# A decoder layer on one core: weight pieces of 128x1024 in place of 128x512, gating in the gates' buffer, expert products kept in fours

## The chip, the cores and the metric

The kernel runs on one core of a Trainium2 chip. The metric is the device time of one execution in microseconds, and lower is better. TensorE (PE, with its weight loads as PEld), VectorE (DVE), ScalarE (ACT), GpSimd (POOL) and SyncE (SP) each run their own instructions in order and wait for one another by semaphores; DMA engines move data between the large memory (HBM) and the on-chip buffers SBUF and PSUM.

## The reference

One decoder layer on 1024 tokens of width 1024, in float32: a hybrid mixer (a gated convolution and a chunked delta rule), cross-attention into 256 memory tokens, and a mixture of 16384 one-neuron experts. The last part sets the size of the work:

```python
def peer_ffn(xn, w_query, sub_keys, expert_u, expert_v):
    ...
    idx = jnp.take_along_axis(cand_idx, pos, axis=-1)
    gates = jax.nn.softmax(best, axis=-1).astype(xn.dtype)
    ...
    def block(args):        
        xt, it, gt = args
        u = expert_u[it]
        v = expert_v[it]
        act = jax.nn.gelu(jnp.einsum("td,ted->te", xt, u), approximate=False)
        return jnp.einsum("te,ted->td", gt * act, v)
```

## The kernel before

The 1024 tokens are eight blocks of 128. They go through the layer in three chunks: `ca` (blocks 0 and 1, 256 tokens), `cb` (blocks 2 to 5, 512 tokens) and `cc` (blocks 6 and 7). The experts are done in two ways. Blocks 0, 1, 6 and 7 fetch the rows that each token chose by indirect DMA, one gather of 128 rows of 4 KB (512 KB) per slot, into a ring `g` of NG = 6 buffers: in `gather_u` VectorE multiplies each with the tokens and sums (line 926, 128 gathers a block, 512 in all), and in `gather_v` VectorE adds it, weighted, to `g_y` (line 1006, 3 blocks). Block 0 goes through `gather_p` instead: TensorE weights and adds the gathered rows. A gather there holds the 128 experts of one token; a pair of gathers is multiplied by two weight columns `W[:, c, u]` in two halves of 512 columns, which makes four products on line 963. The columns land in a strip of 32 of the 128 result rows. There are 64 pairs and 256 products, each of which stands twice in the trace (512 rows).

Blocks 2 to 5 go through all experts instead (`dense`): 32 groups of 512 experts, whose gates were written to the table `gd` in HBM. A group has, in each of its two halves, two calls of `hidden` (line 1066 loads the gates `gv`; a product of 128 experts with 512 tokens, gelu, gating, a split) and one of `output` for the group before it (four result banks, line 1093 adds them to `y`). A group has 192 matmuls of 128x512.

All big products are three matmuls of a split weight and a split input (`mm3`, lines 241 to 243). `load_w` is the path of each weight piece: SP's DMA writes `wraw` (line 233), ACT rounds it to `whi` (line 235), VectorE subtracts to get `wlo` (line 237), and of the three matmuls two read `whi` and one `wlo`. In `proj_ct` (channel-major products and `hidden`) the weights are the stationary operand, in `proj_tok` and `output` they are streamed. A piece is 128x512, so a 128x1024 block of weights is two pieces; there are 904 pieces, in rings of

```python
NSHORT, NRAW, NHI, NLO, NG, LU, LV, VD = 6, 6, 4, 3, 6, 1, 1, 194
```

six, four and three buffers of 2 KB a partition. A ring buffer is written again only when its last reader is done. In `hidden` the gelu goes from PSUM to a short buffer `d_s` (line 1072), VectorE multiplies it with the gates in place (line 1074), ACT rounds it (line 1075) and VectorE subtracts (line 1076); each of these is 128x512 and is done 128 times.

The program is written as generators that `merge` takes steps from in proportion: the gathers of blocks 0 and 1 beside the second chunk, the tables and the third chunk after that, and at the end

```python
run(merge((chain(ga, at('PG3', gathers(6))), 1036 - G1 - G2 - G3 - G4 - G5), (at("PD", dense(2 * P)), PACE)))
```

the remaining gathers beside the dense groups. A scheduler then puts the instructions of each engine into a fixed order by a simulated timeline, so an edit to one instruction can move others.

## Time and profile before

| | us |
|---|---|
| median of 3 runs (lowest, highest) | 3319.79 (3313.24, 3326.74) |
| the profiled execution | 3329.34 |
| its span in the trace | 3327.6 |
| TensorE busy | 2834.6 |
| VectorE busy | 2870.7 |
| POOL, ACT busy | 1275.5, 1169.5 |

The profiled execution is a single one, and 9.6 us longer than the median. Everything read from its trace is set against its own time; the 1.7 us around its span are taken as unchanged. [...] Instructions of one engine overlap a little: the next one on VectorE can start before the end of the one before, so a duration is longer than what an instruction takes from the engine.

### The profile page before, as it was taken

How to read it: one execution, taken by the hardware profiler on the slowest of the kernel's cores; microseconds unless marked ns; L12 is line 12 of the kernel's file. 1: busy time of each engine (PE TensorE's matmuls, PEld its weight loads, DVE VectorE, ACT ScalarE, POOL GpSimd, SP SyncE). 2: the span in 40 equal slices, each digit the busy share in tenths (PEclk: the TensorE clock that was granted, in tenths of full speed). 3: DMA queues.
4: the chain of work that ended last, by engine and by line, in shares of the span. 5: the costliest groups of instructions: out<-in, count | busy, mean ns of one | idle time of the engine just before them, and what ended most of it. 6: DMA issues, size and time to landing. Idle time of an engine off the chain costs nothing.

```text
span 3327.6 us, 45373 instructions
## 1 busy us (share of the span) xinstructions
PE 2834.6 (85%) x14826; PEld 2302.9 (69%) x14826; DVE 2870.7 (86%) x6291; ACT 1169.5 (35%) x2387; POOL 1275.5 (38%) x1028
## 2 busy tenths in 40 slices
PE   8898587868899879464566799899999999999996
PEld 8887566655555556463455677778888888888875
DVE  6665899977665698999999999989999999999996
ACT  5444343312133333333334343233333333333332
POOL 0000036635543433002656154544454454544440
PEclk9899789979999889786778899999999999999998
DMA  4344358948887877214889678999999999989993
GB/s 162 113 133 144 133 199 293 366 164 307 311 298 263 326 257 282 98 59 182 306 293 360 222 258 307 346 309 344 335 345 345 332 347 356 346 317 344 337 338 127
DMA packets 367054, 890.56 MB, mean 268 GB/s; under 512 B 34656, under 2 KB 103904, under 8 KB 362720
## 3 DMA queue, kind: packets, MB, share of 16 engines
q0 software_dynamic: 147456, 536.94, 45.1%
q1 hardware_dynamic: 219360, 350.72, 30.2%
q8 instruction: 116, 1.90, 0.2%
q14 instruction: 122, 1.00, 0.1%
HBM read 838.77 MB, written 48.76 MB: 267 GB/s over the span
## 4 chain that ended last, share of the span: by engine, by line
PE 56%; DVE 23%; DMA 8%; issue 7%; POOL 4%; ACT 2%; SPq 0%; DVEq 0%; POOLq 0%; ACTq 0%
PE ps L241 16%; PE ps L243 16%; PE ps L242 16%; DVE g L926 4%; POOL g L909 3%; DVE wlo L237 2%; PE ps L963 2%; DVE g_y L1006 1%; DMA g<-expert_u,g_ii 1%; DMA wraw<-expert_v 1%; DMA g<-expert_v,g_y 1%; DMA wraw<-u_t 1%; DVE t_s L810 1%; DVE unit L1039 1%; DMA d_s<-kmd 1%
## 5 line engine op out<-in xcount | busy, mean ns | idle before, releaser
L235 ACT ACTIVATE whi<-wraw 128x512 fp32r<-128x512 f32 x904 | 568.5, 632 | 1363.2 <-PE ps L242 599.4
L909 POOL DMA_INDIRECT g<-expert_u,g_ii x512 | 608.2, 1188 | 1020.0 <-DVE t_s L811 443.9
L243 PE MATMUL ps<-unit,wlo 128*128 128x512 f32 (+1 forms) x2144 | 774.6, 365 | 63.7 <-DVE wlo L237 63.6
L909 POOL DMA_INDIRECT g<-expert_v,g_ii x384 | 531.9, 1385 | 774.0 <-DVE g_y L1006 384.2
L237 DVE TENSOR_TENSOR wlo<-wraw,whi 128x512 fp32r<-128x512 f32 x904 | 622.5, 690 | 193.2 <-issue 55.0
L241 PE MATMUL ps<-unit,whi 128*128 128x512 f32 (+1 forms) x2144 | 780.2, 365 | 6.6 <-ACT whi L235 6.0
L242 PE MATMUL ps<-unit,whi 128*128 128x512 f32 (+1 forms) x2144 | 772.1, 361 | 7.9 <-DVE unit L289 7.9
L926 DVE SCALAR_TENSOR_TENSOR g<-g,xn 128x1024 f32<-128x1024 f32 x512 | 622.7, 1222 | 86.9 <-DMA g<-expert_u,g_ii 80.3
L242 PE MATMUL ps<-wlo,unit 128*128 128x512 f32 x1312 | 516.3, 394 | 15.8 <-DVE wlo L237 15.6
L243 PEld LDWEIGHTS ps<-unit,wlo 128*128 128x128 f32 x2144 | 420.9, 197 | 150.7 <-DVE wlo L237 84.7
L243 PE MATMUL ps<-whi,unit 128*128 128x512 f32 x1312 | 513.6, 392 | 0.0
L1006 DVE SCALAR_TENSOR_TENSOR g_y<-g,g_a,g_y 128x1024 f32<-128x1024 f32 x381 | 488.8, 1283 | 9.5 <-DMA g<-expert_v,g_ii 7.9
L241 PEld LDWEIGHTS ps<-unit,whi 128*128 128x128 f32 x2144 | 423.3, 198 | 75.6 <-ACT whi L235 14.3
L242 PEld LDWEIGHTS ps<-unit,whi 128*128 128x128 f32 x2144 | 422.5, 197 | 66.8 <-DVE unit L289 9.2
L241 PE MATMUL ps<-whi,unit 128*128 128x512 f32 x1312 | 411.5, 396 | 18.1 <-ACT whi L235 16.8
L241 PEld LDWEIGHTS ps<-whi,unit 128*128 128x128 f32 x1312 | 247.9, 189 | 79.7 <-ACT whi L235 20.2
L242 PEld LDWEIGHTS ps<-wlo,unit 128*128 128x128 f32 x1312 | 247.7, 189 | 78.4 <-DVE wlo L237 22.4
L243 PEld LDWEIGHTS ps<-whi,unit 128*128 128x128 f32 x1312 | 247.7, 189 | 55.1 <-issue 4.4
L955 POOL DMA_INDIRECT g<-expert_v,g_y x128 | 135.2, 1056 | 173.9 <-DVE g L926 45.4
L963 PE MATMUL ps<-g,g_y 128*32 128x512 f32 x512 | 132.2, 647 | 49.1 <-DMA g<-expert_v,g_y 49.0
L1093 DVE TENSOR_TENSOR unit<-ps,unit 128x512 f32<-128x512 f32 x248 | 162.4, 686 | 11.2 <-PE ps L243 10.9
L1045 PE MATMUL ps<-unit 128*128 128x128 f16 x1024 | 83.6, 239 | 61.0 <-DVE unit L1039 61.0
(276 smaller groups left out, 3062.5 us busy)
## 6 DMA issues: line engine op xcount, KB each, us to landing
wraw<-u_t SPq DMA_DIRECT2D x256, 256.0 KB, 5.5
wraw<-expert_v SPq DMA_DIRECT2D x256, 256.0 KB, 6.4
wraw<-w_in SPq DMA_DIRECT2D x168, 256.0 KB, 4.5
gd<-unit SPq DMA_DIRECT2D x32, 1024.0 KB, 7.9
unit<-gd SPq DMA_DIRECT2D x32, 1024.0 KB, 15.6
wraw<-w_out SPq DMA_DIRECT2D x48, 256.0 KB, 3.5
wraw<-w_xq SPq DMA_DIRECT2D x48, 256.0 KB, 3.9
wraw<-w_xo SPq DMA_DIRECT2D x48, 256.0 KB, 4.2
```

The costliest lines, as they stand in the source:

```text
L235: act(hi, raw, AF.Copy)
L237: tt(lo, raw, hi.bitcast(F32), op=OP.subtract)
L241: nc.tensor.matmul(ps, lh, rh, start=first, stop=False)
L242: nc.tensor.matmul(ps, lh, rl, start=False, stop=False)
L243: nc.tensor.matmul(ps, ll, rh, start=False, stop=last)
L909: nc.gpsimd.indirect_dma_start(out=g, out_offset=None, in_=I[table], in_offset=bass.IndirectOffsetOnAxis(ap=ii[:, k:k + 1], axis=0))
L926: stt(g, g, 1.0, xn, op0=OP.mult, op1=OP.mult, accum_out=r.a[:, k:k + 1])
L955: nc.gpsimd.indirect_dma_start(out=g, out_offset=None, in_=I["expert_v"], in_offset=bass.IndirectOffsetOnAxis(ap=iT[:, t:t + 1], axis=0))
L963: nc.tensor.matmul(acc[32 * cc:32 * cc + 32], W[:, c, u], gs[c][:, half * 512:(half + 1) * 512], start=q == 0 and u == 0, stop=q == 7 and ...
L1006: stt(y, g, a[:, k:k + 1], y, op0=OP.mult, op1=OP.add)
L1045: nc.tensor.matmul(ps[:, u * P:(u + 1) * P], part[i][:, g, :, t], oj[:, g, :, t], start=i == 0, stop=i == 1)
L1093: tt(dst, pss[b], dst, op=OP.add)
```

## The change

Four edits stand together.

1. `load_w` takes 128x1024 at once. There are 452 loads of 512 KB, 452 ACT roundings and 452 subtractions in place of 904 of each. The rings hold 3, 2 and 2 buffers of 4 KB. `proj_tok` and `output` take two row blocks of 512 columns in one load.
2. `hidden` does two blocks of 128 experts: gelu is written back to PSUM, the gating multiplies PSUM with the gates into the gates' buffer `gv`, and one rounding and one subtraction of 128x1024 follow for both.
3. In `gather_p` the four products of a pair of gathers begin with one that needs the later gather, and the other three are tied behind it (`tc.issue_after`).
4. A 128x128 matrix of ones became one column that is read as a broadcast (two small uses, left out of the diff below).

```diff
@@ -43,7 +43,7 @@
 G1, G2, G3, G4, G5 = 98, 90, 107, 17, 137
 A5 = -1
 C4, T5 = 61, 92
-NSHORT, NRAW, NHI, NLO, NG, LU, LV, VD = 6, 6, 4, 3, 6, 1, 1, 194
+NSHORT, NRAW, NHI, NLO, NG, LU, LV, VD = 6, 3, 2, 2, 6, 1, 1, 194
 PG1, PG2, PG3, PT, PR, PD = 100, -25, 0, 0, 0, 0
 
 
@@ -229,11 +229,11 @@
 
     def load_w(src):
 
-        raw = wp.tile([P, 512], F32, name="wraw", bufs=NRAW)
-        nc.sync.dma_start(raw, src)
-        hi = wp.tile([P, 512], F32R, name="whi", bufs=NHI)
+        raw = wp.tile([P, D], F32, name="wraw", bufs=NRAW)
+        nc.sync.dma_start(raw if len(src.shape) == 2 else raw.rearrange("p (a c) -> p a c", a=2), src)
+        hi = wp.tile([P, D], F32R, name="whi", bufs=NHI)
         act(hi, raw, AF.Copy)
-        lo = wp.tile([P, 512], F32R, name="wlo", bufs=NLO)
+        lo = wp.tile([P, D], F32R, name="wlo", bufs=NLO)
         tt(lo, raw, hi.bitcast(F32), op=OP.subtract)
         return hi, lo
 
@@ -296,13 +296,12 @@
 
         xhi, xlo = x
         ps = psum()
-        for g in range(2):
-            hi, lo = load_w(src[:, g * 512:(g + 1) * 512])
-            for j in range(4):
-                k = 4 * g + j
-                js = slice(j * P, (j + 1) * P)
-                mm3(ps[:, :nt], hi[:, js], lo[:, js], xhi[:, k, :nt], xlo[:, k, :nt], k == 0, k == KD - 1)
-            yield
+        hi, lo = load_w(src)
+        for k in range(KD):
+            js = slice(k * P, (k + 1) * P)
+            mm3(ps[:, :nt], hi[:, js], lo[:, js], xhi[:, k, :nt], xlo[:, k, :nt], k == 0, k == KD - 1)
+            if k % 4 == 3:
+                yield
         return ps[:, :nt]
 
     def proj_tok(wsrc, lhs, nblk, consume):
@@ -310,11 +309,14 @@
         for half in range(2):
             pss = [psum() for b in range(nblk)]
             for k in range(KD):
-                hi, lo = load_w(wsrc[k * P:(k + 1) * P, half * 512:(half + 1) * 512])
+                cs = slice(half * 512, (half + 1) * 512)
+                if k % 2 == 0:
+                    hi, lo = load_w(wsrc[k * P:(k + 2) * P, cs].rearrange("(a p) c -> p a c", a=2))
+                ks = slice((k % 2) * 512, (k % 2 + 1) * 512)
                 xh, xl = lhs(k)
                 for b in range(nblk):
                     bs = slice(b * P, (b + 1) * P)
-                    mm3(pss[b], xh[:, bs], xl[:, bs], hi, lo, k == 0, k == KD - 1)
+                    mm3(pss[b], xh[:, bs], xl[:, bs], hi[:, ks], lo[:, ks], k == 0, k == KD - 1)
                 yield
             for b in range(nblk):
                 consume(b, half, pss[b])
@@ -957,13 +959,18 @@
                         gs.append(g)
                         if c == 0:
                             yield
-                    for half in range(2):
-                        for c in range(2):
-                            cc = 2 * c + half
-                            nc.tensor.matmul(acc[32 * cc:32 * cc + 32], W[:, c, u],
-                                             gs[c][:, half * 512:(half + 1) * 512],
-                                             start=q == 0 and u == 0, stop=q == 7 and u == 3,
-                                             skip_group_check=True)
+                    def product(c, half):
+                        cc = 2 * c + half
+                        return nc.tensor.matmul(acc[32 * cc:32 * cc + 32], W[:, c, u],
+                                                gs[c][:, half * 512:(half + 1) * 512],
+                                                start=q == 0 and u == 0, stop=q == 7 and u == 3,
+                                                skip_group_check=True)
+
+
+                    with tc.issue_after(product(1, 0).ins):
+                        product(1, 1)
+                        product(0, 0)
+                        product(0, 1)
                     yield
             st = slip()
             act(st, acc, AF.Copy)
@@ -1066,22 +1073,28 @@
             nc.sync.dma_start(v, gd[:, :, 4 * g:4 * g + 4, :].rearrange("b i j t -> i b j t"))
             return v
 
-        def hidden(g, jj, hh, hl, gv):
-            ps = yield from proj_ct(I["u_t"][4 * g + jj], x, T)
-            a = short()[:, :T]
-            act(a, ps, AF.Gelu)
-            a3 = a.rearrange("p (b t) -> p b t", t=32)
-            tt(a3, a3, gv[:, :, jj, :], op=OP.mult)
-            act(hh[:, jj], a, AF.Copy)
-            tt(hl[:, jj], a, hh[:, jj].bitcast(F32), op=OP.subtract)
+        def hidden(g, j0, hh, hl, gv):
+
+            js = slice(j0, j0 + 2)
+            for jj in (j0, j0 + 1):
+                ps = yield from proj_ct(I["u_t"][4 * g + jj], x, T)
+                act(ps, ps, AF.Gelu)
+                tt(gv[:, :, jj, :], ps.rearrange("p (b t) -> p b t", t=32), gv[:, :, jj, :], op=OP.mult)
+            a = gv[:, :, js, :].rearrange("p b j t -> p j b t")
+            h4, l4 = (h[:, js].rearrange("p j (b t) -> p j b t", t=32) for h in (hh, hl))
+            act(h4, a, AF.Copy)
+            tt(l4, a, h4.bitcast(F32), op=OP.subtract)
 
         def output(g, half, hh, hl):
             pss = [psum() for _ in range(NB)]
             for jj in range(4):
-                vh, vl = load_w(ev[4 * g + jj][:, half * 512:(half + 1) * 512])
+                if jj % 2 == 0:
+                    vh, vl = load_w(ev[4 * g + jj:4 * g + jj + 2, :, half * 512:(half + 1) * 512]
+                                    .rearrange("j i c -> i j c"))
+                vs = slice((jj % 2) * 512, (jj % 2 + 1) * 512)
                 for b in range(NB):
                     bs = slice(b * P, (b + 1) * P)
-                    mm3(pss[b], hh[:, jj, bs], hl[:, jj, bs], vh, vl, jj == 0, jj == 3)
+                    mm3(pss[b], hh[:, jj, bs], hl[:, jj, bs], vh[:, vs], vl[:, vs], jj == 0, jj == 3)
                 yield
             if not y:
                 y.extend(rows(NB))
@@ -1099,8 +1112,7 @@
                 cur = (unit().bitcast(F32R), unit().bitcast(F32R), load_g(g))
             for half in range(2):
                 if cur:
-                    for jj in (2 * half, 2 * half + 1):
-                        yield from hidden(g, jj, *cur)
+                    yield from hidden(g, 2 * half, *cur)
                 if prev:
                     yield from output(g - 1, half, *prev[:2])
             prev = cur
```

How this stands on the engines is read at three places. The first is TensorE at the first products of block 0, beside the delta rule of the second chunk (lines 574 to 626, which are 576 to 628 after the change). `L963` is a product of a gathered pair (`L964` after). Before:

```order
L963 MATMUL ps<-g,g_y 32x512 x3
L595 MATMUL ps<-call,unit 128x128 x8
L963 MATMUL ps<-g,g_y 32x512
L605 MATMUL ps<-unit 128x128 x8
L614 MATMUL ps<-call,unit 128x128 x8
L963 MATMUL ps<-g,g_y 32x512 x3
L623 MATMUL ps<-unit 128x128 x4
L626 MATMUL ps<-unit 128x128 x4
L623 MATMUL ps<-unit 128x128 x3
L963 MATMUL ps<-g,g_y 32x512
L623 MATMUL ps<-unit 128x128
```

After the change:

```order
L964 MATMUL ps<-g,g_y 32x512 x4
L597 MATMUL ps<-call,unit 128x128 x8
L607 MATMUL ps<-unit 128x128 x8
L616 MATMUL ps<-call,unit 128x128 x8
L625 MATMUL ps<-unit 128x128 x2
L964 MATMUL ps<-g,g_y 32x512 x4
L625 MATMUL ps<-unit 128x128 x2
L628 MATMUL ps<-unit 128x128 x4
L625 MATMUL ps<-unit 128x128 x4
L628 MATMUL ps<-unit 128x128 x4
L964 MATMUL ps<-g,g_y 32x512 x4
```

The runs of one and of three products became runs of four. Over the whole program there were 91 runs before, 40 of them of one product, 30 of three and 7 of four; now there are 60, 36 of them of four, 8 of one and 7 of eight.

The second place is VectorE in the first dense groups, from the 444th of the 904 weight pieces on (the 222nd of 452 after the change). `L926` is the multiplication of a gathered row set of `expert_u` for blocks 6 and 7 (`L928` after), `L1006` the addition of one of `expert_v` (`L1013` after), `L885` and its neighbours belong to the routing of block 7, and `L1074` is the gating (`L1082` after). Before:

```order
L237 TENSOR_TENSOR wlo<-wraw,whi 128x512
L926 SCALAR_TENSOR_TENSOR g,g_a<-g,xn 128x1024
L1006 SCALAR_TENSOR_TENSOR g_y<-g,g_a,g_y 128x1024
L237 TENSOR_TENSOR wlo<-wraw,whi 128x512
L885 TENSOR_TENSOR t_s<-t_s,masks 128x1024
L1074 TENSOR_TENSOR d_s<-d_s,unit 128x512
L926 SCALAR_TENSOR_TENSOR g,g_a<-g,xn 128x1024
L237 TENSOR_TENSOR wlo<-wraw,whi 128x512
L1006 SCALAR_TENSOR_TENSOR g_y<-g,g_a,g_y 128x1024
L887 TENSOR_REDUCE p_s_19094<-t_s 128x64
L237 TENSOR_TENSOR wlo<-wraw,whi 128x512
L926 SCALAR_TENSOR_TENSOR g,g_a<-g,xn 128x1024
```

After the change:

```order
L237 TENSOR_TENSOR wlo<-wraw,whi 128x1024
L227 TENSOR_TENSOR rs_t<-rs_t,rs_x 128x1
L928 SCALAR_TENSOR_TENSOR g,g_a<-g,xn 128x1024
L887 TENSOR_TENSOR t_s<-t_s,masks 128x1024
L928 SCALAR_TENSOR_TENSOR g,g_a<-g,xn 128x1024
L237 TENSOR_TENSOR wlo<-wraw,whi 128x1024
L1082 TENSOR_TENSOR unit<-ps,unit 128x16x32
L928 SCALAR_TENSOR_TENSOR g,g_a<-g,xn 128x1024
L228 SCALAR_TENSOR_TENSOR rs_y<-rs_t,rs_y 128x1
L928 SCALAR_TENSOR_TENSOR g,g_a<-g,xn 128x1024
```

The gathered rows stand earlier in the order. Counted from the start of the program, 127 additions of `expert_v` rows stand before the 448th piece in both orders, but of multiplications of `expert_u` rows there were 259 and there are now 275; before the 496th piece there were 320, and there are now 347. Before the 424th piece, still ahead of block 7's rows, there were 112 additions and there are now 119. From the 472nd to the 736th piece the new order is 24 to 27 row sets ahead, counted over both kinds.

The third place is VectorE in the middle of the dense groups, where the two kinds of gathered row sets alternate with the weight pieces. Before (`L1074` and `L1076` are the gating and the split of `hidden`):

```order
L237 TENSOR_TENSOR wlo<-wraw,whi 128x512
L1074 TENSOR_TENSOR d_s<-d_s,unit 128x512
L926 SCALAR_TENSOR_TENSOR g,g_a<-g,xn 128x1024
L237 TENSOR_TENSOR wlo<-wraw,whi 128x512
L1076 TENSOR_TENSOR unit<-d_s,unit 128x512
L1006 SCALAR_TENSOR_TENSOR g_y<-g,g_a,g_y 128x1024
L926 SCALAR_TENSOR_TENSOR g,g_a<-g,xn 128x1024
L237 TENSOR_TENSOR wlo<-wraw,whi 128x512
L1074 TENSOR_TENSOR d_s<-d_s,unit 128x512
L237 TENSOR_TENSOR wlo<-wraw,whi 128x512
L1006 SCALAR_TENSOR_TENSOR g_y<-g,g_a,g_y 128x1024
```

After the change (`L1082` and `L1086` in their place):

```order
L237 TENSOR_TENSOR wlo<-wraw,whi 128x1024
L1082 TENSOR_TENSOR unit<-ps,unit 128x16x32
L928 SCALAR_TENSOR_TENSOR g,g_a<-g,xn 128x1024
L1013 SCALAR_TENSOR_TENSOR g_y<-g,g_a,g_y 128x1024
L928 SCALAR_TENSOR_TENSOR g,g_a<-g,xn 128x1024
L237 TENSOR_TENSOR wlo<-wraw,whi 128x1024
L1082 TENSOR_TENSOR unit<-ps,unit 128x16x32
L1013 SCALAR_TENSOR_TENSOR g_y<-g,g_a,g_y 128x1024
L1086 TENSOR_TENSOR unit<-unit 128x1024
L928 SCALAR_TENSOR_TENSOR g,g_a<-g,xn 128x1024
L237 TENSOR_TENSOR wlo<-wraw,whi 128x1024
L1013 SCALAR_TENSOR_TENSOR g_y<-g,g_a,g_y 128x1024
```

A subtraction is 128x1024 now and stands half as often, the gating reads PSUM, and the split of two blocks of experts is one instruction. On the other engines the order of these steps is the same in kind; the load of `gv` on SP stands after the last `expert_v` piece of a half-group, where it stood before the last `u_t` piece.

## Rows read from the trace of the kernel before

**Rows 1.** The page: busy time by engine, and its chain that ended last.
```profile
PE 2834.6 (85%) x14826; PEld 2302.9 (69%) x14826; DVE 2870.7 (86%) x6291; ACT 1169.5 (35%) x2387; POOL 1275.5 (38%) x1028
...
PE 56%; DVE 23%; DMA 8%; issue 7%; POOL 4%; ACT 2%; SPq 0%; DVEq 0%; POOLq 0%; ACTq 0%
```
**Rows 2.** Windows: length, busy us (instructions) by engine, clock, DMA share, GB/s.
```profile
core 0: us, PE busy (x) PEld busy (x) DVE busy (x) ACT busy (x) POOL busy (x), PEclk, DMA share, GB/s
0.00:332.00 332.00, 291.25 (x1980) 273.91 (x1981) 203.63 (x500) 167.02 (x379) 0.20 (x4) 0.96 0.41 138
500.00:665.00 165.00, 135.74 (x611) 105.67 (x609) 165.00 (x318) 56.13 (x108) 106.34 (x82) 0.95 0.93 329
747.00:1332.00 585.00, 516.73 (x2682) 341.44 (x2682) 417.42 (x1200) 180.91 (x393) 268.74 (x252) 0.92 0.83 292
1332.00:1910.00 578.00, 350.03 (x2595) 305.58 (x2593) 559.71 (x1497) 220.51 (x576) 179.81 (x105) 0.79 0.60 217
1910.00:2240.00 330.00, 311.47 (x1328) 250.79 (x1327) 310.15 (x582) 116.14 (x190) 165.62 (x119) 0.98 0.88 303
2240.00:3160.00 920.00, 918.82 (x4051) 759.90 (x4050) 864.03 (x1236) 302.49 (x514) 451.56 (x382) 1.00 0.96 341
```
**Rows 3.** Waits from 747 to 1332 us: total, times, longest.
```profile
POOL g L909 <- PE ps L963: 103.3, 29, 15.9
...
PE ps L963 <- DMA g<-expert_v,g_y: 49.0, 23, 6.4
```
**Rows 4.** Timeline of TensorE around two runs of products: start, length.
```profile
947.70 1.06 PE L963 MATMUL ps<-g,g_y 128*32 128x512 f32 x6
948.69 0.50 PE L242 MATMUL ps<-unit,whi 128*128 128x512 f32 x1
...
999.63 1.05 PE L963 MATMUL ps<-g,g_y 128*32 128x512 f32 x2
1000.61 0.33 PE L742 MATMUL ps<-call,d_s 128*128 128x128 f32 x1
```
**Rows 5.** Groups by line and form: count, busy us, mean ns, idle before.
```profile
L926 DVE SCALAR_TENSOR_TENSOR g<-g,xn 128x1024 f32<-128x1024 f32 x512 | 622.7, 1222 | 86.9 <-DMA g<-expert_u,g_ii 80.3 <-issue 5.3 <-DMA g<-expert_v,g_y 1.1
L237 DVE TENSOR_TENSOR wlo<-wraw,whi 128x512 fp32r<-128x512 f32 x904 | 622.5, 690 | 193.2 <-issue 55.0 <-ACT whi L235 45.9 <-PE ps L242 44.1
...
L1075 ACT ACTIVATE unit<-d_s 128x512 fp32r<-128x512 f32 x128 | 80.4, 628 | 129.0 <-DVE d_s L1074 128.0
...
L249 ACT ACTIVATE d_s<-unit 128x1024 bf16<-128x1024 f32 x24 | 25.2, 1058 | 9.5 <-DVE unit L334 5.1 <-DMA unit<-x 4.1
```
**Rows 6.** Timeline of VectorE in the dense groups: start, length.
```profile
2401.35 1.22 DVE L926 SCALAR_TENSOR_TENSOR g<-g,xn 128x1024 f32<-128x1024 f32 x1
2402.49 0.09 DVE L926 DVE_READ_ACCUMULATOR g<-g,xn 128x1 f32 x1
2402.49 0.69 DVE L237 TENSOR_TENSOR wlo<-wraw,whi 128x512 fp32r<-128x512 f32 x1
2403.09 1.28 DVE L1006 SCALAR_TENSOR_TENSOR g_y<-g,g_a,g_y 128x1024 f32<-128x1024 f32 x1
```
**Rows 7.** VectorE's subtractions for weight pieces in two stretches (busy, count).
```profile
500.00:665.00 165.00, 28.85 (x42) 0.95 0.93 329
1332.00:2240.00 908.00, 139.47 (x203) 0.86 0.70 248
```
**Rows 8.** The page, DMA issues: count, KB each, us to landing.
```profile
wraw<-u_t SPq DMA_DIRECT2D x256, 256.0 KB, 5.5
wraw<-expert_v SPq DMA_DIRECT2D x256, 256.0 KB, 6.4
...
unit<-gd SPq DMA_DIRECT2D x32, 1024.0 KB, 15.6
```
**Rows 9.** Waits from 2240 to 3160 us: total, times, longest.
```profile
ACT whi L235 <- DMA wraw<-u_t: 109.2, 15, 10.6
ACT unit L1075 <- DVE d_s L1074: 99.5, 57, 3.9
```

8 lines of the change are left out of this document (4 added, 4 removed).

## The prediction

> **What bounds the kernel now.** I read the page first: TensorE is busy 85% of the span and VectorE 86%, so neither is idle enough to be ignored, and the chain that ended last is 56% TensorE and 23% VectorE [rows 1]. An average hides which engine sets the pace where, so the windows come next [rows 2]. The reader should see four kinds of stretch. From 0 to 332 us TensorE works 291 of 332. From 500 to 665 VectorE is busy for all of the 165 us. From 747 to 1332, where block 0's products run, TensorE is the fullest (517 of 585; VectorE 417, DMA 0.83). From 1332 to 1910 VectorE is busy 560 of 578 and TensorE only 350. From 1910 to 2240 both are nearly full (311 and 310 of 330), and from 2240 to 3160 TensorE is busy 919 of 920: there nothing gains time unless it takes matmuls away, and the change takes none. So a gain has to come before 2240, and after 2240 one can only lose. Waits and timelines give the prices.
>
> **Products of block 0.** A run of six rows (three products) that starts at 947.70 is followed by the next matmul at 948.69, and a run of two rows (one product) at 999.63 by the next at 1000.61 [rows 4]. So a run costs 0.98 to 0.99 us whether it holds one product or three. That nothing else runs in most of it is what makes splitting dear. I count this 0.99 for each four products of a run or part of four, an estimate for the longer runs. By the order the old program has 91 runs with 107 such parts, 106 us; the new has 60 with 73, 72 us. TensorE is relieved of 34 us between 747 and 1332. How much comes through? TensorE is at 517/585 = 88% there, which would pass on some 30 us; but in the same stretch TensorE waits 49.0 us for gathered rows inside the runs and POOL waits 103.3 us for products to free a buffer of the ring [rows 3]. A run of four waits for the later of its two gathers and frees both buffers together, so a part of the relief turns into waiting. Bounds 0 and -34; I take two thirds, **-22**.
>
> **Half as many instructions on VectorE.** A subtraction of 128x512 lasts 690 ns, the nearest 128x1024 instruction of two inputs 1222 ns [rows 5]. In the timeline the subtraction that starts at 2402.49 is followed at 2403.09, the 128x1024 one of 2401.35 at 2402.49 [rows 6]: 0.60 and 1.14 us of the engine. A pair saves 2 x 0.60 - 1.14 = 0.06 us. Only stretches that VectorE sets count: 42 + 203 pieces [rows 7], 122 pairs, 7 us. Counted by durations a pair would save 2 x 690 - 1222 = 158 ns and the 122 pairs 19 us, but the starts say that most of this already overlaps the next instruction, and an engine that is full goes by starts. Bounds 0 and -19, taken **-7**. [...] In the dense groups a gating pair drops one more instruction (two splits of 0.60 become one of 1.14), and ACT rounds 1024 in 1058 ns for two times 628 [rows 5]; all of that lies under TensorE's 919 of 920 and counts nothing there.
>
> **Two buffers where there were three or four.** The bytes of the rings stay alike, but a buffer comes free only when a whole 1024 is used. In the first stretch TensorE takes 291.25/1980 = 0.147 us a matmul [rows 2], 3.5 us for the 24 of a pair; the split of the next pair, 1.06 on ACT and 1.22 on VectorE [rows 5], must fit into the time of one: 1.2 us to spare, against 2 x 1.77 - 0.69 = 2.85 before. VectorE is busy 204 of 332 there, so it usually starts at once. There are 76 pairs by the code (28 of the input projection and six times 8). If none is late it costs 0; if each is late by 0.2 us, 15. Nearest is the low end: **+4**.
>
> **Gathered rows earlier in VectorE's order.** By the order, VectorE is 7 gathered row sets ahead of the old program before the 424th piece and 27 before the 496th: 20 more of 1.14 us, 23 us of its time, fall between. This is the stretch 1910 to 2240, in which VectorE is idle 20 us [rows 2]. TensorE's matmuls of the dense groups stand behind the subtractions that these rows delay. DMA also has to bring them sooner: 20 row sets of 0.52 MB are 10.5 MB, 32 GB/s over 330 us on top of 303; that is 335, close to the 341 that the dense stretch moves [rows 2]. Since idle time and bandwidth would both be used to the last, I do not expect it free. Bounds 0 (all of it fills idle time) and +25 (none does, and two us of waits); **+13**, the middle. What is consumed early is missing later, but later VectorE is not the bound, so nothing returns.
>
> **Dense groups with two buffers.** A matmul takes 918.8/4051 = 0.227 us, so TensorE uses a pair up in 5.44 us, and the next pair's split has 5.44 - 1.06 - 1.22 = 3.16 us to spare; before it was 2 x 2.72 - 0.69 = 4.75. How late VectorE takes up a released operation is seen where ACT waits for the gating: 99.5 us in 57 waits, 1.7 on average, 3.9 at most [rows 9]. The mean fits and the longest doesn't. The loads: 5.5 and 6.4 us for 256 KB and 15.6 for 1 MB [rows 8]; 512 KB lie between, and three buffers give 3 x 5.44 = 16.3 us, as six did of 2.72. ACT's 15 waits for `u_t`, up to 10.6 us, cost TensorE nothing before [rows 2, 9]. Bounds 0 and +30 (57 lapses of half a microsecond); **+5**.
>
> In `hidden` the gelu's bank is now held until VectorE has multiplied, some 2 us longer; the eight banks rotate in six allocations a half-group of 96 x 0.227 = 22 us, which covers it. The gates' buffer lives until the split is done, and its next load has most of a group (43 us) against 15.6 [rows 8]. The ones column is nothing.
>
> **Sum.** -22 - 7 + 4 + 13 + 5 = -7 us on the profiled 3329.3, that is 3322; the profile is 9.6 us above the median of the runs, so for the median 3319.8 - 7 = **3313 us**, -0.2%. The measurement can tell about 0.5% (16.6 us) from no change.
>
> **The rivals.** *The relief comes through whole* (0.25). TensorE paces 747 to 1332 and the extra rows only fill the idle 20 us of VectorE and the spare DMA: -34 - 7 + 4 and nothing else, 3283. For it: TensorE is the fullest engine there, and the old runs of one also wait for their own gather. Against it: 49.0 and 103.3 us of waits that a run of four keeps [rows 3], and 1332 to 1910, which VectorE sets and whose work hardly shrinks.
>
> *Slower: the dense groups starve* (0.2). Place: 2240 to 3160 and the groups just before. A subtraction that starts more than 3.16 us after its buffer is free stops TensorE, since the next pair has no other buffer. There are some 225 pairs of weights from 1910 on in that stage; if one in five starts 3.9 us late, the longest seen, each costs 0.74 us: 33 us, and with the other terms 3341; if the wider steps also make VectorE's own lateness grow by half a microsecond, 22 us more, 3363. It decides once VectorE is behind by 3.2 us as a habit, and VectorE is busy 864 of 920 there [rows 2]. Against it: the mean lateness of 1.7.
>
> *VectorE saves by durations* (0.05). If in its full stretches each subtraction holds the next back for its whole 690 ns, every pair saves 158 ns: -22 - 19 + 4 + 13 + 5, 3301. Against it stand the starts in [rows 6]. [...]
>
> *Nothing reaches the end* (0.1). The products' relief is swallowed by gathers and the small terms cancel: 3320. It speaks for this that DMA carries 0.83 between 747 and 1332.
>
> **How the numbers follow.** The forecast has 0.4, with a range of its own from 3295 to 3338; of that 0.26 lies within 0.5% (3303 to 3336), 0.12 below and 0.02 above. Faster: 0.12 + 0.25 of the first rival + 0.04 of the third = 0.41. Slower: 0.2 + 0.02 = 0.22. The same: 0.26 + 0.1 + the third's 0.01 = 0.37. The range goes down to 3270 (the first rival with VectorE's 19 us would be 3271) and up to 3346 (the starving case at its first price), leaving out one in ten on either side.
>
> **What would show it.** In the new profile: runs of eight product rows, about 60 of them, and TensorE's busy time in block 0's stretch down by some 30 us; a subtraction group of 452 with a mean near 1.22 us; the start of the full-TensorE stretch at about 2235, and earlier if the first rival holds; in that stretch TensorE still busy over 99%, and its waits for `wlo` near zero, or tens of microseconds if it starves. If the first dense groups take longer than their 330 us, the early rows are the cause. The prediction is wrong if the products' stretch shortens by less than 10 us, or if the last 1100 us change their length by more than 15.

## The result, and the profile after

The changed kernel takes 3350.28 us (median of 4 runs, 3345.26 to 3353.46), the kernel before 3316.92 (4 runs). The ratio is 1.0095, with a 95% interval of 1.0067 to 1.0122: slower by 0.7 to 1.2%, where 3313 us was forecast, 0.2% faster, which is less than the measurement can tell from no change. The profiled execution of the changed kernel has a span of 3350.7 us, 23.1 us more than that of the kernel before. That one was about 12 us above the median of its runs, so the two traces locate 23 of the 33 us by which the medians differ.

The page of the changed kernel: busy time by engine, the chain that ended last, and two groups, the subtractions and the products. They answer to [rows 1] and [rows 5].

```profile
PE 2807.9 (84%) x14826; PEld 2315.4 (69%) x14826; DVE 2832.8 (85%) x5775; ACT 1080.4 (32%) x1871; POOL 1362.3 (41%) x1028
...
PE 39%; DVE 13%; DMA 4%; issue 4%; POOL 1%; ACT 1%; SPq 0%; DVEq 0%; ACTq 0%; POOLq 0%
...
L237 DVE TENSOR_TENSOR wlo<-wraw,whi 128x1024 fp32r<-128x1024 f32 x452 | 551.4, 1221 | 187.6 <-ACT whi L235 184.4
...
L964 PE MATMUL ps<-g,g_y 128*32 128x512 f32 x512 | 87.1, 692 | 71.7 <-DMA g<-expert_v,g_y 71.4
```

TensorE's matmuls, VectorE and ACT are busy for less time than before (26.7, 37.9 and 89.1 us less), and the kernel is longer. The shares of this chain add up to 62% of the span and those before to 100%, so the two can't be set against each other. The windows, to be read against [rows 2] (length, busy us and instructions by engine, clock, DMA share, GB/s):

```profile
0.00:332.00 332.00, 287.82 (x1973) 270.51 (x1974) 194.05 (x432) 153.41 (x311) 0.21 (x4) 0.97 0.40 136
500.00:665.00 165.00, 139.66 (x616) 112.22 (x615) 162.26 (x294) 52.15 (x88) 107.92 (x82) 0.90 0.91 324
747.00:1332.00 585.00, 474.92 (x2627) 340.94 (x2628) 402.38 (x1110) 166.92 (x335) 286.48 (x254) 0.88 0.82 293
1332.00:1910.00 578.00, 345.06 (x2573) 301.25 (x2572) 557.22 (x1457) 210.16 (x526) 184.60 (x105) 0.77 0.58 215
1910.00:2240.00 330.00, 307.26 (x1275) 243.76 (x1274) 315.33 (x558) 102.79 (x118) 177.16 (x131) 0.96 0.89 316
2240.00:3160.00 920.00, 920.00 (x4061) 761.78 (x4060) 856.73 (x1013) 267.90 (x302) 510.54 (x383) 1.00 0.96 343
```

Three things stand in them. From 747 to 1332 TensorE's busy time fell from 517 to 475 us, but the row also holds 55 fewer of its matmuls, so a part of that is work done later. From 1910 to 2240 there are 53 fewer matmuls, at 0.227 us each 12 us of work that is done later. From 2240 to 3160 TensorE is busy all the time; the dense groups do not starve there.

Fixed windows hold different work in the two kernels, so the comparison needs stretches of equal work. The trace of each holds 3456 matmuls that read `wlo`, so the ends of number 720, 1200, 1480, 2000 and of the last, counted from 0, cut every kernel into the same work. In the kernel before they end at 642.3, 1363.2, 1925.0, 2307.5 and 3302.3 us. The table gives how much longer (+) or shorter (-) each stretch is than there, worked out from these ends in each trace. "VectorE full" is the stretch from number 1200 to 1480. The rows below the changed kernel are the runs of the next section.

| kernel | to 720 | products, to 1200 | VectorE full, to 1480 | first dense groups, to 2000 | rest |
|---|---|---|---|---|---|
| before, us | 642.3 | 720.9 | 561.8 | 382.5 | 994.8 |
| changed | +2.3 | +3.2 | +10.9 | +12.7 | -5.8 |
| e1_products | +2.0 | +16.6 | -1.5 | -9.1 | +8.3 |
| e2_pieces | -0.8 | +0.1 | +7.2 | +18.7 | -0.5 |
| e3_gating | -2.9 | -2.5 | -0.5 | -10.9 | -6.0 |
| e4_no_products | +0.3 | +0.5 | +9.7 | +15.2 | -1.4 |
| e5_halves44 | -12.2 | +2.5 | -1.7 | -10.4 | +15.0 |
| e5_halves43 | -1.9 | +21.7 | +8.5 | +19.4 | +3.1 |
| e7_halves_old_products | -16.0 | +3.4 | 0.0 | -3.5 | +3.2 |
| b_lo2 | +31.1 | -9.7 | +11.4 | +57.7 | +54.4 |
| e8_ng7 | +12.3 | -9.6 | +6.9 | +71.4 | +115.3 |
| e9_gating_lo4 | -5.3 | 0.0 | +3.6 | -21.3 | -6.0 |
| e10_hi2_lo3 | +31.4 | -1.5 | +10.6 | +11.1 | -6.0 |
| e11_hi3_lo2 | +31.6 | -8.7 | +0.3 | -9.3 | +11.1 |
| e12_gating_ng7 | +28.2 | -29.6 | +3.0 | +9.6 | -6.0 |
| e13_gating_ng7_products | +35.7 | -32.0 | +1.0 | +18.0 | -6.0 |
| e14_gating_lo4_products | +0.8 | -7.6 | +1.3 | -20.8 | -6.0 |

The reader sees where the 23 us are: 10.9 where VectorE is full and 12.7 in the first dense groups. The products' stretch, from which 22 us were to come, gave nothing. The -6.0 that six kernels share is the last stretch without a wait (in e9_gating_lo4 TensorE is busy 989.00 of 989 us from 2284 to 3273).

There is one trace of each kernel, and single executions differ: those of the kernel before lie between 3300.83 and 3326.29 us in one set of 18. An entry below some 10 us may thus be the draw of one execution. The trace of the kernel before is itself about 12 us above the median; e1_products, which leaves the dense groups alone, is 9.1 us shorter in the first of them. What is read below rests on entries that return in several kernels, or on medians.

The same stretches in numbers, the kernel before first (ends rounded to whole us): the products' stretch, VectorE full, the first dense groups.

```profile
642.00:1363.00 721.00, 602.70 (x3254) 421.19 (x3253) 537.52 (x1571) 214.60 (x471) 314.87 (x290) 0.90 0.77 273
1363.00:1925.00 562.00, 346.84 (x2539) 300.88 (x2539) 543.71 (x1342) 220.62 (x575) 183.48 (x107) 0.79 0.61 223
1925.00:2307.00 382.00, 363.47 (x1557) 293.85 (x1557) 358.33 (x651) 129.04 (x214) 192.48 (x143) 0.98 0.90 313
```

```profile
645.00:1369.00 724.00, 568.88 (x3273) 428.71 (x3272) 524.60 (x1500) 204.88 (x421) 330.84 (x289) 0.86 0.76 270
1369.00:1941.00 572.00, 351.66 (x2530) 303.58 (x2529) 550.69 (x1305) 212.99 (x529) 194.55 (x113) 0.78 0.62 227
1941.00:2337.00 396.00, 373.26 (x1566) 298.42 (x1565) 371.90 (x605) 117.83 (x135) 219.00 (x162) 0.97 0.92 327
```

In the products' stretch TensorE does 34 us less, as forecast, and the stretch is 3 us longer. In the other two VectorE does 7.0 and 13.6 us more, although it has fewer instructions there. The gathered row sets say why: by the traces VectorE starts 110 of them in the first of the two stretches instead of 103, and 162 in the second instead of 144, and from start to start one takes 1.14 us (`expert_u`, [rows 6]) or 1.20 (`expert_v`, from 2403.09 to 2404.29 us in the kernel before). This count separates the kernels of the table. The kernel before has 247 row sets in the two stretches together; the seven others with 240 to 251 are 3.5 to 19.5 us shorter there, the seven with 263 to 276 (the changed kernel has 272) are 13 to 28 us longer, and b_lo2 with 289 and e8_ng7 with 299 are 69 and 78 us longer. The order is fixed before the kernel runs, so a longer stretch doesn't draw these rows in; the counts before the 496th piece, given with the expectations, say the same.

### The profile page after: what moved, and what is told of

It is laid out like the page before. It is cut to its first block, busy times and chain, and to the rows that moved or that the text cites. A ratio compares the mean times of both kernels' runs of the same rounds, so it can differ in the third digit from the quotient of the medians.

```text
span 3350.7 us, 42421 instructions
## 1 busy us (share of the span) xinstructions
PE 2807.9 (84%) x14826; PEld 2315.4 (69%) x14826; DVE 2832.8 (85%) x5775; ACT 1080.4 (32%) x1871; POOL 1362.3 (41%) x1028
## 4 chain that ended last, share of the span: by engine, by line
PE 39%; DVE 13%; DMA 4%; issue 4%; POOL 1%; ACT 1%; SPq 0%; DVEq 0%; ACTq 0%; POOLq 0%
PE ps L243 13%; PE ps L242 13%; PE ps L241 13%; DVE unit L1046 1%; DVE g_y L1013 1%; DVE wlo L237 1%; DMA wraw<-expert_v 1%; POOL g L911 1%; DVE unit L1043 1%; DVE unit L1044 1%; DVE g L928 1%; DMA g<-expert_v,g_ii 1%; DMA gd<-unit 1%; DMA g<-expert_u,g_ii 1%; DVE t_s L812 1%
## 5 line engine op out<-in xcount | busy, mean ns | idle before, releaser
L911 POOL DMA_INDIRECT g<-expert_u,g_ii x512 | 661.5, 1292 | 944.5 <-DVE t_s L813 461.7
L235 ACT ACTIVATE whi<-wraw 128x1024 fp32r<-128x1024 f32 x452 | 479.3, 1061 | 1322.4 <-PE ps L242 641.0
L911 POOL DMA_INDIRECT g<-expert_v,g_ii x384 | 561.9, 1463 | 727.3 <-DVE g_y L1013 350.0
L241 PE MATMUL ps<-unit,whi 128*128 128x512 f32 (+1 forms) x2144 | 786.2, 367 | 18.6 <-ACT whi L235 18.6
L928 DVE SCALAR_TENSOR_TENSOR g<-g,xn 128x1024 f32<-128x1024 f32 x512 | 618.4, 1218 | 156.2 <-DMA g<-expert_u,g_ii 133.1
L237 DVE TENSOR_TENSOR wlo<-wraw,whi 128x1024 fp32r<-128x1024 f32 x452 | 551.4, 1221 | 187.6 <-ACT whi L235 184.4
L243 PE MATMUL ps<-whi,unit 128*128 128x512 f32 x1312 | 515.9, 393 | 0.0
L1013 DVE SCALAR_TENSOR_TENSOR g_y<-g,g_a,g_y 128x1024 f32<-128x1024 f32 x381 | 487.1, 1279 | 5.3 <-DMA g<-expert_v,g_ii 3.3
L241 PE MATMUL ps<-whi,unit 128*128 128x512 f32 x1312 | 448.5, 395 | 10.2 <-ACT whi L235 9.3
L243 PEld LDWEIGHTS ps<-whi,unit 128*128 128x128 f32 x1312 | 249.0, 190 | 54.4 <-issue 2.9
L964 PE MATMUL ps<-g,g_y 128*32 128x512 f32 x512 | 87.1, 692 | 71.7 <-DMA g<-expert_v,g_y 71.4
```

The lines of the kernel that those rows point to most:

```text
L235: act(hi, raw, AF.Copy)
L237: tt(lo, raw, hi.bitcast(F32), op=OP.subtract)
L241: nc.tensor.matmul(ps, lh, rh, start=first, stop=False)
L243: nc.tensor.matmul(ps, ll, rh, start=False, stop=last)
L911: nc.gpsimd.indirect_dma_start(out=g, out_offset=None, in_=I[table], in_offset=bass.IndirectOffsetOnAxis(ap=ii[:, k:k + 1], axis=0))
L928: stt(g, g, 1.0, xn, op0=OP.mult, op1=OP.mult, accum_out=r.a[:, k:k + 1])
```

## The experiments

**One edit at a time.** The products alone:

```diff
-                    for half in range(2):
-                        for c in range(2):
...
+                    with tc.issue_after(product(1, 0).ins):
+                        product(1, 1)
+                        product(0, 0)
+                        product(0, 1)
```

> The kernel before with the edit of the products alone (69 runs of 83 parts of four, against 91 of 107). Theory A, that the stretch from 747 to 1332 us is paced by the gathers that the products wait for: TensorE's busy time on the products falls by about 30 us, its waits for gathered rows rise by nearly as much, and the time stays within 6 us of before. Theory B, that TensorE paces this stretch and the relief was lost elsewhere in the changed kernel: 15 to 24 us faster than before.

Measured: 3340.03 us against 3315.88, ratio 1.0065 (1.0041 to 1.0089). Neither theory: it is slower, and 16.6 of the loss is in the products' own stretch. The stretch from 644 to 1382 us of this run, and its waits:

```profile
644.00:1382.00 738.00, 577.99 (x3257) 426.44 (x3256) 533.76 (x1571) 213.89 (x471) 319.82 (x290) 0.87 0.76 266
```

```profile
DVE g L926 <- DMA g<-expert_u,g_ii: 115.2, 62, 8.6
...
PE ps L962 <- DMA g<-expert_v,g_y: 64.6, 15, 8.9
```

VectorE's wait before, from 642 to 1363 us:

```profile
DVE g L926 <- DMA g<-expert_u,g_ii: 78.0, 55, 10.2
```

TensorE is busy 578.0 us, where the same work took 602.7 before: 25 us of it are gone. Its waits for gathered rows in this stretch went from 49.0 [rows 3] to 64.6, and VectorE's for the other gathers from 78.0 to 115.2. So the time taken from TensorE became waiting for gathers. That is what theory A said of the relief; it did not foresee a loss.

The pieces alone:

```diff
-NSHORT, NRAW, NHI, NLO, NG, LU, LV, VD = 6, 6, 4, 3, 6, 1, 1, 194
+NSHORT, NRAW, NHI, NLO, NG, LU, LV, VD = 6, 3, 2, 2, 6, 1, 1, 194
...
-        raw = wp.tile([P, 512], F32, name="wraw", bufs=NRAW)
+        raw = wp.tile([P, D], F32, name="wraw", bufs=NRAW)
```

> The pieces of 128x1024 alone, with the old products and the old gating. Its order on VectorE has the gathered rows early as in the changed kernel (349 multiplications of expert_u rows before the 496th piece, against 320 before and 347 in the changed kernel). Theory A, that the pieces bring the whole loss, half of it by this order in the first dense groups: 25 to 38 us slower than before, with about 15 us of it between the 400th and the 460th piece. Theory B, that the loss comes from the three edits together or from the gating: under 12 us slower.

Measured: 3354.20 us, ratio 1.0107 (1.0074 to 1.0140), 38 us slower. Theory A: the pieces alone lose as much as the whole change, and the trace has 18.7 us of it in the first dense groups. VectorE takes 272 row sets in the two stretches, as in the changed kernel.

The gating alone:

```diff
-            a = short()[:, :T]
-            act(a, ps, AF.Gelu)
...
+                act(ps, ps, AF.Gelu)
+                tt(gv[:, :, jj, :], ps.rearrange("p (b t) -> p b t", t=32), gv[:, :, jj, :], op=OP.mult)
```

> The gating in the gates' buffer alone. Its order has the gathered rows within 5 of those of the kernel before. Theory A: the dense stretch is paced by TensorE and hides this edit, within 6 us of before. Theory B, that the longer hold of the PSUM bank and the later split hold TensorE up: 10 to 30 us slower, with waits of TensorE in the dense stretch.

Measured: 3310.77 us, ratio 0.9984 (0.9970 to 0.9998). Theory A: 5 us faster. The trace of this run is 23 us shorter than that of the kernel before, 10.9 of it in the first dense groups, but the medians of the two kernels differ by 5, so most of these 10.9 us are the draw of two executions and not shown to be the edit's.

The changed kernel with the old products:

```diff
-                    with tc.issue_after(product(1, 0).ins):
-                        product(1, 1)
...
+                    for half in range(2):
+                        for c in range(2):
```

> The changed kernel with the old products. Theory A, that the products' edit is worth nothing: 26 to 38 us slower than before, within 6 us of the changed kernel. Theory B, that it is worth 15 to 24 us and hides a larger loss: 45 to 58 us slower than before.

Measured: 3351.88 us, ratio 1.0102 (1.0075 to 1.0129). Theory A: in the changed kernel the products' edit is worth nothing (its stretch +3.2 with it, +0.5 without).

**Is it the size of the load, or the rings of the split?** The rings of the split are those of the rounded pieces (`whi`) and the subtracted ones (`wlo`). The loads stay at 512 KB, but rounding and subtraction go by halves, in rings of four and four 2 KB buffers:

```diff
-NSHORT, NRAW, NHI, NLO, NG, LU, LV, VD = 6, 3, 2, 2, 6, 1, 1, 194
+NSHORT, NRAW, NHI, NLO, NG, LU, LV, VD = 6, 3, 4, 4, 6, 1, 1, 194
...
+        for i in range(2):
+            r = raw[:, i * 512:(i + 1) * 512]
+            hi = wp.tile([P, 512], F32R, name="whi", bufs=NHI)
+            act(hi, r, AF.Copy)
+            lo = wp.tile([P, 512], F32R, name="wlo", bufs=NLO)
+            tt(lo, r, hi.bitcast(F32), op=OP.subtract)
```

> The changed kernel with loads of 512 KB, but each load rounded and subtracted in two halves of 128x512, in rings of four and four 2 KB buffers (as many bytes as two and two of 4 KB). Its order has 314 multiplications of expert_u rows before the 496th piece (320 before, 347 in the changed kernel). Theory A, that the coarse split rings let the gathered rows run ahead in VectorE's order and that this is the loss: the first dense groups take no longer than before, and the time is between 10 us below and 12 us above that of the kernel before. Theory B, that the large loads or their three raw buffers are the loss: 25 to 38 us slower than before.

Measured: 3326.91 us against 3317.45, ratio 1.0035 (1.0015 to 1.0056). Theory A: the two stretches that lost 10.9 and 12.7 are now 1.7 and 10.4 us shorter than before, with 240 row sets in them instead of 272. Finer split rings undo the loss there although the loads stay large. That doesn't make large loads free: this run has four subtracted buffers where the kernel before had three, and it loses 15.0 in the rest of the dense groups, which the theory did not name. What the loads cost is read below, at e14_gating_lo4_products.

The same with one buffer less:

```diff
-NSHORT, NRAW, NHI, NLO, NG, LU, LV, VD = 6, 3, 4, 4, 6, 1, 1, 194
+NSHORT, NRAW, NHI, NLO, NG, LU, LV, VD = 6, 3, 4, 3, 6, 1, 1, 194
```

> The same with three buffers for the subtracted halves instead of four; 338 multiplications of expert_u rows stand before the 496th piece. Theory A: 8 to 20 us slower than with four, most of it in the first dense groups. Theory B: the same time as with four, within 5 us.

Measured: 3381.13 us, ratio 1.0188 (1.0156 to 1.0221), 54 us slower than with four and not 8 to 20. The direction is that of theory A; the size is nearly three times the upper end of what was expected, and the products' stretch loses 21.7 too. Its split rings are four and three, as in the kernel before, so these rings with large loads are far from free.

With the old products and rings of four and four, against e5_halves44:

```diff
-                    with tc.issue_after(product(1, 0).ins):
-                        product(1, 1)
...
+                    for half in range(2):
+                        for c in range(2):
```

> Loads of 512 KB with split halves in rings of four and four, the new gating, and the old products: 318 multiplications of expert_u rows before the 496th piece. Theory A: as fast as the gating alone or a little faster, 3 to 15 us faster than before. Theory B: 20 to 35 us slower than before.

Measured: 3325.33 us, ratio 1.0021 (1.0006 to 1.0036): not 20 to 35 us slower, so theory B is out, but not faster either. Halves with a 512 KB load are no gain over the kernel before.

The kernel before, unchanged but for the ring of subtracted pieces:

```diff
-NSHORT, NRAW, NHI, NLO, NG, LU, LV, VD = 6, 6, 4, 3, 6, 1, 1, 194
+NSHORT, NRAW, NHI, NLO, NG, LU, LV, VD = 6, 6, 4, 2, 6, 1, 1, 194
```

> The kernel before, pieces of 128x512 and all, with two buffers for the subtracted pieces instead of three. Its order has 366 multiplications of expert_u rows before the 496th piece. Theory A, that a short ring alone does it: 15 to 40 us slower than before, most of it between the 400th and the 500th piece. Theory B: within 6 us of before.

Measured: 3463.81 us, ratio 1.0420 (1.0380 to 1.0459): 146 us, far beyond either. One 2 KB buffer is worth more than everything that the change does, and VectorE's order has 46 more `expert_u` rows before the 496th piece. TensorE's waits in its first dense groups (1958 to 2398 us):

```profile
PE ps L241 <- ACT whi L235: 24.5, 6, 10.0
PE ps L242 <- DVE wlo L237: 18.3, 12, 3.6
PE ps L243 <- DVE wlo L237: 15.0, 13, 2.1
```

**Which ring?** The changed kernel with three 4 KB buffers in one of the two. The bytes come from two short buffers (`NSHORT` 4). All four runs that give them up are 28 to 36 us longer before number 720 (the column "to 720"), so these runs are read by stretch.

```diff
-NSHORT, NRAW, NHI, NLO, NG, LU, LV, VD = 6, 3, 2, 2, 6, 1, 1, 194
+NSHORT, NRAW, NHI, NLO, NG, LU, LV, VD = 4, 3, 2, 3, 6, 1, 1, 194
```

> The changed kernel with three 4 KB buffers for the subtracted pieces and two for the rounded ones (and four short buffers instead of six). Its order stays as in the changed kernel, 346 multiplications of expert_u rows before the 496th piece. Theory H, that the two rounded buffers are the short link: within 8 us of the changed kernel, 26 to 42 us slower than before. Theory L, that the two subtracted buffers are (what the prediction's bound was worked out for): 5 to 20 us slower than before.

Measured: 3362.75 us against 3319.28, ratio 1.0130 (1.0094 to 1.0165): 43 us slower, a little above theory H's range and far from theory L's.

```diff
-NSHORT, NRAW, NHI, NLO, NG, LU, LV, VD = 6, 3, 2, 2, 6, 1, 1, 194
+NSHORT, NRAW, NHI, NLO, NG, LU, LV, VD = 4, 3, 3, 2, 6, 1, 1, 194
```

> The changed kernel with three 4 KB buffers for the rounded pieces and two for the subtracted ones (and four short buffers instead of six). Its order has 324 multiplications of expert_u rows before the 496th piece. Theory H: 0 to 18 us slower than before, the first dense groups within 6 us of before. Theory L: as the changed kernel, 26 to 42 us slower than before.

Measured: 3343.56 us, ratio 1.0078 (1.0050 to 1.0106). The first dense groups of both, the run with the third subtracted buffer first:

```profile
1966.00:2359.00 393.00, 369.38 (x1562) 294.40 (x1561) 371.82 (x605) 115.85 (x133) 221.52 (x163) 0.98 0.93 330
```

```profile
1948.00:2321.00 373.00, 360.08 (x1559) 293.53 (x1558) 354.29 (x577) 113.29 (x130) 205.68 (x146) 0.99 0.91 320
```

The same 1560 matmuls take 393 and 373 us. POOL did 163 and 146 instructions in them, VectorE 605 and 577: with the third rounded buffer 17 gathers fewer have moved into this stretch. By the table the third rounded buffer takes back 10.6 and 22.0 us of the two stretches that lost, set against the changed kernel; the third subtracted one 0.3 and 1.6. Both traces are 11 to 12 us above the medians of their kernels, which differ by 19 us, so the difference between the two runs stands. Theory H. The total with the third rounded buffer, though, is not within 0 to 18 us: the 31.6 us before number 720 and another 11 in the rest stand against it.

**The order, without the rings.** Seven gather buffers bring the gathered rows forward with the split rings of before. First in the kernel before, with two raw buffers given up for it:

```diff
-NSHORT, NRAW, NHI, NLO, NG, LU, LV, VD = 6, 6, 4, 3, 6, 1, 1, 194
+NSHORT, NRAW, NHI, NLO, NG, LU, LV, VD = 6, 4, 4, 3, 7, 1, 1, 194
```

> The kernel before with seven gather buffers instead of six and four raw buffers instead of six; the rings of the split pieces stay at four and three. Its order has 352 multiplications of expert_u rows before the 496th piece (320 before), and 388 before the 520th (349). Theory O, that gathered rows ahead in VectorE's order are by themselves what costs: 12 to 30 us lost between the 400th and the 520th piece. Theory R, that short split rings cost by TensorE waiting for them, and the order only shows it: under 8 us lost there.

Measured: 3524.96 us, ratio 1.0623 (1.0584 to 1.0661), beyond both theories, with 115 us lost in the rest. Four raw buffers (`wraw`) instead of six are the likelier reason: in the first dense groups ACT waits 142.8 us for pieces of `u_t` to land, 40.8 in the kernel before, and from there to the end the DMA share is 0.78. By itself this run can't tell them from the order. Then with the gating and all six raw buffers:

```diff
-NSHORT, NRAW, NHI, NLO, NG, LU, LV, VD = 6, 6, 4, 3, 6, 1, 1, 194
+NSHORT, NRAW, NHI, NLO, NG, LU, LV, VD = 4, 6, 4, 3, 7, 1, 1, 194
```

> The gating alone with seven gather buffers instead of six (and four short buffers instead of six); split rings four and three, raw ring six, as before. 349 multiplications of expert_u rows stand before the 496th piece, as in the changed kernel (347; the gating alone has 325). Theory O, that gathered rows ahead of the pieces cost by themselves: the first dense groups take 10 to 20 us longer than with the gating alone, with waits of TensorE for split pieces. Theory R, that only the short split rings cost: within 5 us of the gating alone in that stretch. The short buffers cost some 20 to 40 us before the products' stretch in either case, as in the two runs with four of them.

Measured: 3334.87 us against 3318.64, ratio 1.0067 (1.0044 to 1.0090). The first dense groups of this run, and of the gating alone:

```profile
1927.00:2319.00 392.00, 372.42 (x1563) 295.04 (x1563) 378.97 (x674) 128.78 (x199) 211.24 (x165) 0.98 0.95 335
```

```profile
1919.00:2291.00 372.00, 361.21 (x1562) 293.34 (x1561) 360.42 (x643) 126.90 (x197) 180.72 (x147) 0.99 0.94 327
```

Theory O: 18 more gathers in the stretch, and 20.5 us more by the table, with split rings as in the kernel before. VectorE is at 97% in both and does 18.6 us more, so the extra rows are paid in full. With as many rows ahead as e8_ng7 this run is 16 us slower than the kernel before, and not 206; it differs from that run by the raw buffers, the gating and two short buffers.

The same run shows something else. The products' stretch, from 671 to 1362 us, is 29.6 us shorter than before:

```profile
671.00:1362.00 691.00, 593.86 (x3253) 418.02 (x3252) 504.23 (x1514) 214.99 (x472) 294.12 (x263) 0.91 0.75 264
```

```profile
DVE g L926 <- DMA g<-expert_u,g_ii: 49.3, 30, 8.7
PE ps L963 <- DMA g<-expert_v,g_y: 42.8, 21, 4.7
```

TensorE's busy time is only 9 us less than the 602.7 of before, and still the stretch is 30 us shorter, what 25 us less work on TensorE did not do in e1_products. Two things came together: a seventh gather in flight, and 27 gathers fewer in the stretch (POOL 263 against 290 instructions), because the stretch ahead of it, 28 us longer, had already done them. This run doesn't separate the two. b_lo2 comes nearest: it has as few gathers (POOL 264) with six buffers, and its stretch is 9.7 us shorter. Either way the stretch goes by its gathers.

**Products with deeper rings.** The run e12_gating_ng7 with the products kept together:

```diff
-                    for half in range(2):
-                        for c in range(2):
...
+                    with tc.issue_after(product(1, 0).ins):
+                        product(1, 1)
```

> The same with the four products of a pair kept together. Theory G, that the gathers in flight pace the products' stretch: with the seventh buffer a held pair costs less, and this run is within 6 us of the one without the products' edit in that stretch, not 16 slower. Theory T, that a run of four costs by standing in TensorE's order ahead of ready work: 10 to 20 us slower there than without it, seven buffers or six.

Measured: 3346.80 us, ratio 1.0102 (1.0075 to 1.0130). The products' stretch of this run:

```profile
678.00:1367.00 689.00, 563.33 (x3255) 424.91 (x3255) 505.21 (x1517) 215.20 (x475) 285.73 (x263) 0.89 0.75 265
```

Theory G: 30.5 us less work on TensorE and 2.4 us less time; no loss. Its whole time is 12 us longer all the same, 7.5 of it before the products begin and 8.4 in the first dense groups.

The gating alone with a fourth buffer for the subtracted pieces, from one of the six short buffers that the new gating no longer needs:

```diff
-NSHORT, NRAW, NHI, NLO, NG, LU, LV, VD = 6, 6, 4, 3, 6, 1, 1, 194
+NSHORT, NRAW, NHI, NLO, NG, LU, LV, VD = 5, 6, 4, 4, 6, 1, 1, 194
```

> The gating alone, with four buffers for the subtracted pieces instead of three (the 2 KB come from one of six short buffers, which the new gating no longer needs). 319 multiplications of expert_u rows stand before the 496th piece. If deeper rings help: 6 to 25 us faster than before. If three were enough: as the gating alone, 0 to 8 us faster.

Measured: 3299.39 us against 3319.28 (10 and 14 runs), ratio 0.9942 (0.9927 to 0.9957). Deeper rings help: 20 us with the gating, which alone gave 5. Its first dense groups:

```profile
1923.00:2284.00 361.00, 356.54 (x1563) 292.17 (x1562) 354.40 (x634) 127.33 (x196) 180.20 (x142) 1.00 0.94 328
```

TensorE is busy 357 of 361 us; this stretch has little more to give. And the same with the products kept together:

```diff
-                    for half in range(2):
-                        for c in range(2):
...
+                    with tc.issue_after(product(1, 0).ins):
+                        product(1, 1)
```

> The fastest version so far (gating, four subtracted buffers) with the four products of a pair kept together. If the products' edit is worth nothing anywhere: within 6 us of that version. If it is worth its relief of TensorE once the rings are deep enough: 10 to 25 us faster. If it costs as when done alone: 12 to 25 us slower.

Measured: 3298.23 us, ratio 0.9946 (0.9928 to 0.9965): worth nothing, though it doesn't cost. Both beat the kernel before by half a percent and the changed one by 1.5%.

These two runs also price the large loads. e9_gating_lo4 and e7_halves_old_products have the same gating, the same products and split rings of four and four 2 KB buffers; they differ in the loads (256 KB into six raw buffers, or 512 KB into three), in one short buffer and in the matrix of ones. So do e14_gating_lo4_products and e5_halves44, with the products kept together. Set against its own kernel before, each by its medians, the first pair is at -20 and +8 us and the second at -20 and +9: the large loads are 28 and 30 us slower. VectorE takes 246 and 245 row sets in the two stretches, so the order isn't the reason. In the first dense groups ACT waits longer for raw pieces, in e9_gating_lo4 and then in e7_halves_old_products:

```profile
ACT whi L235 <- DMA wraw<-expert_v: 25.9, 5, 9.6
```

```profile
ACT whi L248 <- DMA wraw<-expert_v: 73.9, 13, 12.5
```

Whether the size of a load or the raw ring of three makes this difference isn't separated, and no run has it for the changed kernel, which loses nothing in the rest of the dense groups.

## Why the prediction was wrong

Its sum was -7 us, and the traces show +23. Two steps failed. The products' stretch, taken at -22, came out at +3.2, and the stretch where VectorE is full, taken at -7, came out at +10.9: 25 and 18 of the 30 us between. By its terms:

**Products, -22 taken, 0 to -34 as bounds.** This is the step that failed first. TensorE's relief was as large as worked out: 34 us in the stretch, and the group of the product rows fell from 132.2 us before, here, to 87.1.

```profile
L963 PE MATMUL ps<-g,g_y 128*32 128x512 f32 x512 | 132.2, 647 | 49.1 <-DMA g<-expert_v,g_y 49.0
```

But that TensorE at 88% "would pass on some 30 us" took a busy share for a pace. In five pairs of kernels the edit changed the products' stretch by +16.6 (e1_products against before), +2.7 (changed against e4_no_products), -0.9 (e5_halves44 against e7_halves_old_products), -2.4 (e13_gating_ng7_products against e12_gating_ng7) and -7.6 (e14_gating_lo4_products against e9_gating_lo4): the mean is near zero. By medians of the whole time the same pairs are at +24, -3, +2, +12 and -1 us; none is faster beyond noise. The waits of the changed kernel from 747 to 1340 us answer to [rows 3]:

```profile
DVE g L928 <- DMA g<-expert_u,g_ii: 124.6, 56, 10.7
...
PE ps L964 <- DMA g<-expert_v,g_y: 71.4, 16, 8.9
...
POOL g L911 <- PE ps L964: 62.4, 23, 12.4
```

POOL waits less for TensorE (103.3 before), and TensorE and VectorE wait more for gathers (49.0 and 75.6 us before, from 747 to 1332): the gathers set the pace, and a run of four only moves where its wait stands. The 49.0 and 103.3 us that stood against the first rival were the decisive rows, and I gave them a third of the weight. Why the edit costs 16.6 us when done alone is open; in the four other pairs it did not.

**VectorE's saving, -7.** The stretch where VectorE is full became 7 to 11 us longer with the pieces (e2_pieces, e4_no_products, changed), not shorter. The instruction is as foreseen. Here it is in the dense groups of the changed kernel, 1.23 us long, with the next start 1.14 us later:

```profile
2401.88 1.23 DVE L237 TENSOR_TENSOR wlo<-wraw,whi 128x1024 fp32r<-128x1024 f32 x1 [0.52 <-ACT whi L235]
2403.02 0.68 DVE L1082 TENSOR_TENSOR unit<-ps,unit 128x512 f32<-128x512 f32 x1
```

What swallowed the saving are seven row sets: I had counted them, "7 gathered row sets ahead of the old program before the 424th piece", and given them no price. At 1.20 us they are some 8 us of VectorE in a stretch that it sets, and it is busy 7.0 us longer there. By the durations a merged pair saves 2 x 690 - 1221 = 159 ns; by the starts, 0.60 us before [rows 6] and 1.14 here, it saves the 0.06 us of the prediction.

**Two buffers, +4 in the first stretch and +5 in the dense one.** Both places were wrong: the first stretch lost 2.3 us, the last stretch nothing, and the two between, 10.9 and 12.7. Nor did the loss there come about as reckoned, by TensorE waiting for a late split: its waits in the first dense groups are 22.5 us, and 18.5 before. The longest, in the changed kernel and then before:

```profile
PE ps L241 <- ACT whi L235: 11.5, 16, 2.9
PE ps L243 <- DVE wlo L237: 9.8, 5, 2.4
```

```profile
PE ps L241 <- ACT whi L235: 13.1, 4, 4.8
```

VectorE waits for the rounded piece instead (184.4 us in the whole run, 45.9 before [rows 5]), and the order is another one. Of the two rings it is the rounded one that is short, which the slack of 3.16 us did not tell apart: the third rounded buffer took back 10.6 and 22.0 us, the third subtracted one 0.3 and 1.6.

**Gathered rows earlier, +13.** Right in mechanism: the stretch lost 12.7 us and took 18 row sets more, and e12_gating_ng7 shows rows as far ahead to cost 20.5 with the split rings unharmed. That 13 and 12.7 agree is in part luck, since the trace of the kernel before is a long one: against e3_gating, which has the order of before but for five rows, the changed kernel is 23.6 us longer in that stretch, near the upper bound of 25. What I missed is the cause and the other stretch. I took the order as given, and it follows from the rings: with a third rounded buffer 324 of the `expert_u` rows stand before the 496th piece instead of 347. How much of the loss in the changed kernel is the order and how much a direct wait for a split piece isn't separated, since one ring sets both.

**The gating, 0.** It was said to lie under TensorE's 919 of 920 us, and nearly does: alone it gave 5 us, with an interval that ends just short of no change, and on top of the pieces 2 (e4_no_products against e2_pieces, by medians), which is within noise. Its worth is the short buffer that it frees.

**The rivals.** "The dense groups starve" had the sign. Its main place lost nothing (from 2240 to 3160 the changed kernel's TensorE is busy 920.00 of 920), and in "the groups just before" TensorE's waits grew by 4 us only. "The relief comes through whole" is out. The forecast's range ended at 3346, 4 us below the result: no case let the largest gain be zero while two stretches lost, which is what happened. And the large loads, reasoned to cost nothing because three buffers give 16.3 us, cost 28 to 30 us where the split rings were equal; what they cost in the changed kernel is open.
